# The experts' gates as one float32r product of N=256 per token, in place of three bf16 products

## The chip, the cores and the metric

The kernel runs on one core of one Trainium2 chip, as one program of some 47,000 recorded instructions. The metric is device time in microseconds from the program's start to its end; the time before is the median of three runs.

Names in what follows: PE is the TensorE (matrix products, results in PSUM), DVE the VectorE, ACT the ScalarE, POOL the GpSimd engine, SP the SyncE, which issues the loads of weights.

## The reference, cut to what matters

The program is one transformer block on 256 tokens: a modulated norm, a gated delta net and a sparse attention side by side, an output product, then a layer of 16384 small experts (PEER). The change lies in the last part alone:

```python
# 8 heads, 128 x 128 keys, 16 experts per head and token: 128 slots per token
s1 = einsum('thd,hkd->thk', qh[..., :half], keys1); v1, i1 = top_k(s1, 16)
s2 = einsum('thd,hkd->thk', qh[..., half:], keys2); v2, i2 = top_k(s2, 16)
sc, pos = top_k(v1[..., :, None] + v2[..., None, :], 16)      # over the 256 pairs
eidx = take_along_axis(i1 * 128 + i2, pos)                    # expert = (i, j)
gw = softmax(sc)                                              # the gates
act = gelu(einsum('td,thkd->thk', xb, u[eidx]))
out = einsum('thk,thkd->td', gw * act, v[eidx])
```

Only 128 of the 16384 experts have a gate that isn't zero for a given token.

## The kernel before

The kernel computes the activations of all 16384 experts densely, times a gate that is mostly zero, and then multiplies with all of v. Expert (i, j) lies in partition i, column j of two tiles A0 (j below 80) and A1 (the rest), each [128, js, 256 tokens].

*The loop over j (lines 1886 to 1901).* For each of 128 j, `stat256` makes 48 products of 128x256 on PE: 16 blocks of the model's width, three float32r passes each (the weights u in two parts, the activations in two parts). ACT applies gelu into A. The weights come through `Stream`, 512 KB a load, each load cut into two pieces of 128x512. ACT casts a piece to its high part `whi`, DVE subtracts to give the low part `wlo`; each piece feeds 12 products, so a j takes four. There are four buffers of each part (line 1636), and a piece is split when one is given out:

```python
stream = Stream(jobs2, 4, 4)                          # line 1636
S.copy(h[:, :n], r)                                   # advance(): whi
V.tensor_tensor(l[:, :n], r, h[:, :n], OP.subtract)   # wlo
```

*The gates (`gate_task`, lines 1827 to 1883)* run beside that loop, four tokens at a time in 64 batches. For a token t, G[i, j] = sum over the 128 slots of gate * [i = i_slot] * [j = j_slot]: a product over slots of two tables, `oi` (one where i is the slot's) and `ow` (the gate where j is the slot's). `make` builds the tables of a batch on DVE: two comparisons of 128x512 bf16 and three multiplications, since the gate is held in three bf16 parts whose sum is exact. `products` makes 12 products of 128x128 bf16, three accumulated per token. `put` multiplies the gates into the part of A that is there (DVE), and copies them to where activations are still to come (ACT); there the loop multiplies later (`aj`, lines 1896 to 1898).

*What sets the order.* The program is written out in one order by hand; each engine runs its own instructions in that order and waits on semaphores. `Background` advances generators between the products with u: after each three products `bg.step()` lets each chain go on if the planner's estimated time on PE (`times.free["P"]`) has come. `pause()` (line 1835) spaces a batch's four steps evenly over the time left until the loop's end less GEND = 20 us; a step yields a time, which is a lower bound beside the estimated end of the last instructions (plain), or the only condition (with a minus). After the loop `need("gates")` (line 1902) runs whatever steps are left, and only then the second half follows: products with v, whose left operand `wh`, `wl` is A split in two.

The routing before it (`route_task`) ends with the transposed tables of i, j and gate, slots in partitions, and the flag "gate", for which `gate_task` waits.

Of the kernel before, what the change touches and what calls it, by code (L numbers as in the profile page):

```python
# [18 lines left out]
T = 256  # L19
# [48 lines left out]
def _const_array():  # L68
# [19 lines left out]
    # inside chunks of 64, both of a block's by their rows  # L88
# [21 lines left out]
def _ktiled(w, width):  # L110
    """[K, N] -> flat, by column chunks of `width`: [N/width][K/256][128][2][width]"""
    K, N = w.shape
    return w.reshape(K // 256, 2, 128, N // width, width).transpose(3, 0, 2, 1, 4).reshape(-1)


def layout(i):
    """Arrays for the device: the inputs, laid out anew."""
# [61 lines left out]
# h comes in slices of its columns: the first block of 128, and how many  # L179
SLICES = [(0, 1), (1, 1)] + [(2 * i, 2) for i in range(1, 8)]  # L180
PART = "ma0 mb0 ma1 mb1 ma2".split()
ORDER = "vcvs h1 h2 h3 h4 h5 h6 h7 ma0 mb0 kskw vw ma1 mb2 mb1 ma2".split()   # under the delta net
CMP_AT = "h2 h3 h4 h5 h6 h7 kskw vw".split()
COVER_N = [["ma3"], ["mb3", "wg0"], ["wg1", "wg2"], ["wg3"]]    # under the sparse attention
# [6 lines left out]
class Times:  # L191
    """A rough estimate of when the instructions emitted so far will have run, in microseconds. It says only
    when a chain goes on between the long products; no result rests on it."""
# [3 lines left out]
    def __init__(self):  # L197
        self.free = dict.fromkeys([*"PVSGQD", "DQ"], 0.0)   # engines, the queue of loads, DMA, that for the queue
        self.by, self.ready, self.used = {}, {}, {}     # by tile: its writer, when it is written and was last used
        self.slots, self.array = {}, []  # L200
        self.mark, self.table = 0.0, 0
# [28 lines left out]
    def beside(self, lhsT, out):  # L230
        """in rows or columns of the array that the products just before leave free?"""
        r, c = lhsT.start_partition(), out.start_partition()
        new = r, r + lhsT.partition_size(), c, c + out.partition_size()
        if self.array and all(new[1] <= o[0] or o[1] <= new[0] or new[3] <= o[2] or o[3] <= new[2] for o in self.array):
            self.array.append(new)
            return True
        self.array = [new]
        return False
# [37 lines left out]
class Timed:  # L276
    """An engine whose instructions are noted in times."""
# [30 lines left out]
class Background:  # L308
    """Chains of short dependent steps, advanced between the long products: generators that yield where the
    next step needs the results of the last. What they yield, if anything, is a time to wait for besides, or,  # L310
    with a minus, instead."""

    def __init__(self, times, cap, fill, pace):
        """fill(): side work that waits for nothing; one piece of it each `pace()`"""
# [39 lines left out]
class Tokens:  # L354
    """Buffers that a chain may hold from one of its steps to another."""
# [13 lines left out]
class Lanes:  # L369
    """Sets of buffers, of which a chain takes one."""  # L370
# [13 lines left out]
def build(nc, tc, A, out, dump=None, stop=None):  # L384
    """dump(name, ap): a hook for debugging"""
# [17 lines left out]
def _build(nc, tc, A, out, stacks, dump, at, stop_at):  # L403
# [35 lines left out]
    banks = Tokens(6)       # of the 8: those that are held for longer than a step  # L439
# [8 lines left out]
    # ------------------------------------------------------------ the stream of weights  # L448
    class Stream:
        """Tiles of 128 x 1024 or less, loaded and given out in the order of jobs; a tile to be split comes  # L450
        as two halves, each in two float32r parts."""

        def __init__(self, jobs, nraw, nsplit, more=None, nmore=0, until=0):
            """jobs: (array, offset, elements by partition, pieces to be split, the step from one partition to
            the next if it isn't the elements'); 0 pieces: one that isn't split; for those before `until` there is also
            the room of nmore tiles in the pool `more`"""
# [7 lines left out]
            self.got = 0            # pieces given out  # L464
            # by pool: of how many tiles, and how many are loaded, neither split nor given out
            self.room, self.open_raw = [(self.raws, nraw), (more, nmore)], [0, 0]
            self.until = until
            self.open_cut = 0       # pieces split, not given out
            self.held = False       # the last piece given out is a raw tile
            self.hold = False       # split nothing for now  # L470
# [14 lines left out]
        def advance(self, busy):  # L485
            """busy: split pieces that are in use"""
            self.load()
            while len(self.ready) < len(self.pieces):
# [10 lines left out]
                r = self.raw[i][:, hf * n:(hf + 1) * n]     # the last of them frees it  # L499
# [10 lines left out]
        def get(self):  # L510
            """The next piece; the one before must have been used."""
# [15 lines left out]
    # ------------------------------------------------------------ constants  # L527
# [14 lines left out]
    mcol = cst.tile([128, 6, KT], F32, name="mcol")   # sh1, norm1_w (1 + sc1), g1, sh2, norm2_w (1 + sc2), g2  # L542

    modr = dram.tile([2, D], F32, name="modr")        # g1, g2
# [3 lines left out]
    # ------------------------------------------------------------ plan of the front's stream  # L548
# [7 lines left out]
    def jobs_ks(n, ks):  # L556
        """a pair of ks of a chunk, or one of them"""
# [3 lines left out]
    def jobs_ada(sl):  # L561
        """shift, then scale"""
# [4 lines left out]
    # shift, scale and gate of the first half, then of the second  # L567
    SH1, SC1, G1, SH2, SC2, G2 = range(6)
    cmp_left = [(A["cw1"], i * 128 * 1024, 1024, 0) for i in range(16)]
    # Until the whole of sh1 and sc1 is there, a slice of h is used as soon as it can be: for two chunks, whose  # L570
    # sums stay in PSUM, and for some of the mixers, whose sums go through DRAM. The tiles of ada for the next
    # slice come between those.
    LEAVE = SLICES[-1][0] // 2          # the first tile of a chunk that comes after
    jobs = jobs_ada(0)
    order = []                  # of the steps: (slice, chunk, ks) or "ada"
    for sl, (k0, nk) in enumerate(SLICES[:-1]):
# [6 lines left out]
        for i, n in enumerate(steps):  # L583
# [6 lines left out]
            else:  # L590
                order.append("ada")         # the end of the slice, by steps
# [5 lines left out]
    # after which tiles of which chunks one for the compressed keys and values comes  # L597
# [23 lines left out]
    # of W_out the last quarter in two: the less is left to do when the products are done  # L621
# [11 lines left out]
    st_f = stack()          # left: what the front keeps  # L633

    # the rest of what is loaded once
# [8 lines left out]
    # ------------------------------------------------------------ products in three float32r passes  # L644
# [3 lines left out]
    def dense(accs, lhi, llo, w, ks, first, last, name=None, ready=None):  # L648
        """accs[tb][128 tokens, w] = sum from the first k to the last of lhs^T(k, tb) weights(k, w)"""
# [19 lines left out]
    # ------------------------------------------------------------ ada  # L669
    def ada_tile(p, i, n, r):  # L670
        """p: rows 0, 32, 64, 96 add up to n blocks of 128 columns; the i-th tile of them"""
# [20 lines left out]
    def c_row(dst):  # L692
        """silu(c) in every partition"""
# [7 lines left out]
    def ada_late(parts, crow, acol, row, room):  # L701
        """parts of ada, by step 512 terms of 128 columns; crow(q): 512 of c's; room(m): where the m-th piece comes"""
# [39 lines left out]
    def ada_until(*parts):  # L742
        """the side work up to the end of some parts"""
# [8 lines left out]
    # ------------------------------------------------------------ h = norm(x) (1 + sc1) + sh1, transposed  # L752
# [110 lines left out]
    # ------------------------------------------------------------ gates, decays, rotary angles  # L863
# [12 lines left out]
    rc = per.tile([128, 2, 32], F32, name="rc")       # cos | cos  # L876
    rs = per.tile([128, 2, 32], F32, name="rs")       # -sin | sin
    gg = per.tile([128, 2, 8], F32, name="gg")
    Gc = per.tile([128, 2, 8], F32, name="Gc")        # cumulated g
    nGc = per.tile([128, 2, 8], F32, name="nGc")  # L880
    gam = per.tile([128, 2, 8], F32, name="gam")      # exp(G)
    bgm = per.tile([128, 2, 8], F32, name="bgm")      # beta exp(G)
    ekd = per.tile([128, 2, 8], F32, name="ekd")      # exp(G_end - G)
    ge = per.tile([128, 4, 8], F32, name="ge")        # exp(G_end) by chunk, in every partition
    kcT = per.tile([128, 2, 2, T], F32, name="kcT")   # k_c, v_c: [d, which, group, t]
    beta = sig[:, :, 8:16]
    # by head and chunk (of a block's two, one in each half of the partitions): exp(-|G_i - G_j|)
# [3 lines left out]
    def pre_task():  # L891
        # what is needed until E is written, in its place
# [18 lines left out]
        # angles brought into [-pi, pi]  # L911
# [23 lines left out]
        # g = -exp(A_log) softplus(a + dt_bias), cumulated inside chunks of 64  # L935
# [52 lines left out]
    def rope(dst, src, tb, n):  # L988
        """the first 32 of dst [128 t, n heads, 128] = those of src, rotated"""
# [13 lines left out]
    def kv_rot(a, o, dst, free):  # L1003
        """rotated and transposed columns [o, o + 256) of a chunk: dst [128 d, 2 groups, T]"""
# [19 lines left out]
    # ------------------------------------------------------------ gated delta net, a head at a time  # L1024
# [3 lines left out]
    # (I + L)^-T of a block, both chunks'; between them stays 0  # L1028
# [8 lines left out]
    def gdn_head(h, a):  # L1037
# [28 lines left out]
        # q and k stay as they are: 1 / |k| goes into the scales of what is made of them and into the rows of  # L1066
        # (I + L)^-1, which then gives U / |k| instead of U; 1 / |q| into the output's scale
# [981 lines left out]
```

## Time and profile before

| | |
|---|---|
| median of 3 runs (lowest, highest) | 2715.28 us (2714.2, 2716.81) |
| span of the profiled execution | 2713.1 us (no time of its own is given beside it) |
| PE, DVE, ACT busy | 99%, 72%, 51% of the span |
| loop over u | some 1161 to 1984 us |
| gates, first to last table and product | 1358.6 to 1913.4 us |
| products with v | from 1984.4 us |

The profile's views read here: the page's engine totals and its chain of work that ended last; windows (busy time of each engine in a stretch); groups of equal instructions with their mean duration; and timelines, in which the idle time ahead of an instruction stands in brackets with what ended it. A line number of a helper (L286) stands at nearly every instruction, so instructions are told apart by their tiles: `ps` is a PSUM bank, `ht` holds the activations h2. An instruction's duration reaches beyond the start of the next on its engine, so what one occupies is read from the distance of starts.

### The profile page before, as it was taken

How to read it: one execution, taken by the hardware profiler on the slowest of the kernel's cores; microseconds unless marked ns; L12 is line 12 of the kernel's file. 1: busy time of each engine (PE TensorE's matmuls, PEld its weight loads, DVE VectorE, ACT ScalarE, POOL GpSimd, SP SyncE). 2: the span in 40 equal slices, each digit the busy share in tenths (PEclk: the TensorE clock that was granted, in tenths of full speed). 3: DMA queues.
4: the chain of work that ended last, by engine and by line, in shares of the span. 5: the costliest groups of instructions: out<-in, count | busy, mean ns of one | idle time of the engine just before them, and what ended most of it. 6: DMA issues, size and time to landing. Idle time of an engine off the chain costs nothing.

```text
span 2713.1 us, 47110 instructions
## 1 busy us (share of the span) xinstructions
PE 2675.2 (99%) x17132; PEld 2275.8 (84%) x17132; DVE 1956.5 (72%) x4360; ACT 1389.9 (51%) x2966; POOL 35.2 (1%) x77
## 2 busy tenths in 40 slices
PE   7999999999999999999999999999999999999998
PEld 5777767777777777999999999999988888788886
DVE  6667877767777777899766666667577777766666
ACT  4446656555554445554544444444455555555555
POOL 0000000000000000000000000000000000000000
PEclk9999999999999999999999999999999999999999
DMA  9886756676676886566655555555577777766664
GB/s 345 311 314 213 223 166 202 209 235 218 208 238 203 306 301 210 188 180 186 184 159 157 154 156 156 156 155 156 174 250 234 235 236 236 255 188 187 188 189 158
DMA packets 176922, 571.12 MB, mean 211 GB/s; under 512 B 20049, under 2 KB 20385, under 8 KB 176177
## 3 DMA queue, kind: packets, MB, share of 16 engines
q1 hardware_dynamic: 168336, 538.18, 62.8%
q0 software_dynamic: 6624, 23.65, 2.5%
q10 hardware_dynamic: 1728, 6.29, 0.6%
q8 instruction: 134, 2.20, 0.3%
q14 instruction: 100, 0.81, 0.1%
HBM read 554.91 MB, written 13.13 MB: 209 GB/s over the span
## 4 chain that ended last, share of the span: by engine, by line
PE 93%; DVE 3%; DMA 2%; ACT 1%; issue 1%; DVEq 0%; ACTq 0%; POOLq 0%
PE ps L286 93%; DMA adas<-ada_t 1%; DVE wlo L286 1%; DVE adas L286 0%; DMA raw<-w_in 0%; ACT whi L286 0%; DVE x L286 0%; DVE ht L286 0%; DMA ccom<-consts 0%; DMA mix<-partd 0%; DVE big L286 0%; ACT P L286 0%; DMA mixd<-mix 0%; ACT ps L286 0%; ACT mix L286 0%
## 5 line engine op out<-in xcount | busy, mean ns | idle before, releaser
L286 DVE TENSOR_TENSOR wlo<-raw,whi 128x512 fp32r<-128x512 f32 (+2 forms) x1632 | 1099.8, 685 | 521.7 <-ACT whi L286 487.6
L286 ACT CAST whi<-raw 128x512 fp32r<-128x512 f32 (+2 forms) x1632 | 995.1, 618 | 778.8 <-PE ps L286 622.0
L286 PE MATMUL ps<-ht,whi 128*128 128x256 f32 x4608 | 828.8, 282 | 0.8 <-DVE ht L286 0.8
L286 PEld LDWEIGHTS ps<-ht,whi 128*128 128x128 f32 x4608 | 708.1, 189 | 1.2 <-DVE ht L286 1.0
L286 PE MATMUL ps<-ht,wlo 128*128 128x256 f32 x2304 | 647.2, 281 | 0.0
L286 PE MATMUL ps<-whi,ht 128*128 128x512 f32 (+2 forms) x1536 | 527.5, 402 | 4.4 <-ACT whi L286 2.7
L286 PEld LDWEIGHTS ps<-ht,wlo 128*128 128x128 f32 x2304 | 434.1, 188 | 0.0
L286 PE MATMUL ps<-wlo,wh 128*128 128x512 f32 x1024 | 406.0, 396 | 0.0
L286 PE MATMUL ps<-whi,wl 128*128 128x512 f32 x1024 | 405.0, 396 | 0.0
L286 PE MATMUL ps<-whi,wh 128*128 128x512 f32 x1024 | 402.6, 393 | 0.8 <-ACT wh L286 0.8
L286 PEld LDWEIGHTS ps<-whi,ht 128*128 128x128 f32 x1536 | 286.9, 188 | 91.2 <-issue 14.8
L286 PE MATMUL ps<-wlo,ht 128*128 128x512 f32 (+2 forms) x768 | 298.3, 388 | 2.2 <-DVE wlo L286 2.0
L286 PEld LDWEIGHTS ps<-whi,wh 128*128 128x128 f32 x1024 | 192.2, 188 | 48.9 <-ACT wh L286 1.0
L286 PEld LDWEIGHTS ps<-wlo,wh 128*128 128x128 f32 x1024 | 192.2, 188 | 47.0
L286 PEld LDWEIGHTS ps<-whi,wl 128*128 128x128 f32 x1024 | 192.2, 188 | 45.3 <-DVE wl L286 0.2
L286 ACT CAST wh<-A 128x256 fp32r<-128x256 f32 x256 | 103.9, 407 | 134.0 <-PE ps L286 134.0
L286 PEld LDWEIGHTS ps<-wlo,ht 128*128 128x128 f32 x768 | 145.2, 189 | 27.4 <-DVE wlo L286 4.9
L286 DVE TENSOR_TENSOR wl<-A,wh 128x256 fp32r<-128x256 f32 x256 | 108.8, 426 | 64.9 <-ACT wh L286 64.5
L286 DVE SCALAR_TENSOR_TENSOR adas<-adas,crow 128x512 f32<-128x512 f32 x192 | 131.4, 684 | 29.2 <-DMA adas<-ada_t 28.9
L286 PE MATMUL ps<-ow,oi 128*128 128x128 bf16 x768 | 101.3, 296 | 0.0
L286 ACT COPY A<-ps 128x192 f32<-128x192 f32 (+16 forms) x124 | 34.4, 307 | 114.0 <-DVE A L286 93.3
L286 PEld LDWEIGHTS <-oi 128*128 128x128 bf16 x768 | 81.7, 118 | 3.9
(320 smaller groups left out, 2307.3 us busy)
## 6 DMA issues: line engine op xcount, KB each, us to landing
raw<-u SPq DMA_DIRECT2D x256, 512.0 KB, 3.6
raw<-v SPq DMA_DIRECT2D x256, 512.0 KB, 3.6
raw<-w_in SPq DMA_DIRECT2D x170, 512.0 KB, 4.3
adas<-ada_t SPq DMA_DIRECT2D x192, 256.0 KB, 3.6
raw<-ada_w SPq DMA_DIRECT2D x64, 512.0 KB, 6.8
raw<-wn SPq DMA_DIRECT2D x32, 512.0 KB, 4.8
raw<-wo SPq DMA_DIRECT2D x32, 512.0 KB, 5.0
raw<-wq SPq DMA_DIRECT2D x32, 512.0 KB, 3.6
```

The lines of the kernel that those rows point to most:

```text
L286: r = f(*args, **kw)
```

## The change

The gate is now held in two parts, a float32r rounding and the rest, and both tables are float32r. For each token one product of N=256 gives the sums of both parts side by side, which then have to be added. In full:

- `make` builds the tables by token: `tensor_scalar` over a 128-column bf16 iota with the slot's i, j and gate parts as scalars per partition. That is one instruction for `oi` and two for `ow`, 12 of 128x128 per batch in two halves of two tokens, and four small ones per batch (`sl`, `gr`) that lay out the scalars. The tables have three buffers each, of two tokens.
- `products` makes four products of 128x256 float32r per batch, two tokens to a PSUM bank.
- `put` goes by two tokens: ACT copies one part from PSUM to the tile `gsum` (one buffer), DVE adds the other, and then the multiplication into A or the copies follow from `gsum`.
- The order of the steps in `gate_task` is written anew, four to a batch as before; the routing's split of the gate in three goes; `aj` has one buffer instead of two.

```diff
-    ij = [ep.tile([128, T], BF, name=f"ij{n}") for n in range(2)]
-    gs = [ep.tile([128, T], BF, name=f"gs{n}") for n in range(3)]
-    iota4 = ep.tile([128, 128, 4], BF, name="iota4")
+    ij = ep.tile([128, 2, T], BF, name="ij")
+    gs = ep.tile([128, T], F32, name="gs")
+    iotab = ep.tile([128, 128], BF, name="iotab")
...
         def make(t0):
-            oi = ep.tile([128, 128, nt], BF, name="oi", bufs=2)
-            ow = ep.tile([128, 3, 128, nt], BF, name="ow", bufs=2)
-            over = lambda a: a[:, None, t0:t0 + nt].to_broadcast([128, 128, nt])
-            V.tensor_tensor(ow[:, 2], iota4, over(ij[1]), OP.is_equal)
-            V.tensor_tensor(oi, iota4, over(ij[0]), OP.is_equal)
-            yield -pause()
-            for n in range(3):
-                V.tensor_tensor(ow[:, n], ow[:, 2], over(gs[n]), OP.mult)
-            ones[t0] = oi, ow
+            sl = ep.tile([128, 4, nt], F32, name="sl", bufs=2)
+            gr = ep.tile([128, nt], F32R, name="gr", bufs=2)
+            gt = gs[:, t0:t0 + nt]
+            V.tensor_copy(sl[:, 0:2], ij[:, :, t0:t0 + nt])
+            V.tensor_copy(gr, gt)
+            V.tensor_copy(sl[:, 2], gr)
+            V.tensor_tensor(sl[:, 3], gt, gr, OP.subtract)
+            ones[t0] = []
+            for i in range(nt // 2):
+                if i:
+                    yield -pause()
+                oi = ep.tile([128, 2, 128], F32R, name="oi", bufs=3)
+                ow = ep.tile([128, 2, 2, 128], F32R, name="ow", bufs=3)
+                for t in range(2):
+                    at = [sl[:, n, 2 * i + t:2 * i + t + 1] for n in range(4)]
+                    V.tensor_scalar(oi[:, t], iotab, at[0], None, op0=OP.is_equal)
+                    for n in range(2):
+                        V.tensor_scalar(ow[:, t, n], iotab, at[1], at[2 + n], op0=OP.is_equal, op1=OP.mult)
+                ones[t0].append((oi, ow))

         def products(t0):
-            for t in range(nt):
-                for n in range(3):
-                    PE.matmul(p[:, 128 * t:128 * t + 128], oi[:, :, t], ow[:, n, :, t], start=n == 0, stop=n == 2)
+            for oi, ow in ones.pop(t0):
+                p = ps()
+                for t in range(2):
+                    PE.matmul(p[:, 256 * t:256 * t + 256], oi[:, t], ow[:, t].rearrange("p n j -> p (n j)"),
+                              start=True, stop=True)
+                sums[t0].append(p)

         def put(t0):
-            pv = sums.pop(t0).rearrange("p (t j) -> p j t", t=nt)
...
+            for i, p in enumerate(sums.pop(t0)):
+                g = ep.tile([128, 128, 2], F32, name="gsum", bufs=1)
+                pv = p.rearrange("p (t n j) -> p n j t", t=2, n=2)
+                S.copy(g, pv[:, 1])
+                V.tensor_tensor(g, g, pv[:, 0], OP.add)
+                for q, (a, b) in enumerate(((0, JA), (JA, 128))):
+                    m = min(max(j_there, a), b)
+                    x = act_by[q][:, :, t0 + 2 * i:t0 + 2 * i + 2]
+                    if m > a:
+                        V.tensor_tensor(x[:, :m - a], x[:, :m - a], g[:, a:m], OP.mult)
+                    if m < b:
+                        S.copy(x[:, m - a:], g[:, m:b])
...
         for t0 in range(0, T, nt):
-            if t0 + nt < T:
-                yield from make(t0 + nt)
-                yield -pause()
+            new = make(t0 + nt) if t0 + nt < T else None
+            if new:
+                yield next(new)
             if t0:
                 put(t0 - nt)
             yield pause()
             products(t0)
+            yield -pause()
+            if new:
+                next(new, None)
             yield pause()
```

On DVE, a batch in the middle of the stage, before (A_11574 is A0; `ps` in the row on A is the bank of the gates' sums; `aj` is gelu's result where gates are there already):

```order
L286 TENSOR_TENSOR ow<-iota_11582,ij_11578 128x512
L286 TENSOR_TENSOR oi<-iota_11582,ij_11577 128x512
L286 TENSOR_TENSOR wlo<-raw,whi 128x512
L286 TENSOR_TENSOR ow<-ow,gs_11579 128x512
L286 TENSOR_TENSOR ow<-ow,gs_11580 128x512
L286 TENSOR_TENSOR ow<-ow,gs_11581 128x512
L286 TENSOR_TENSOR wlo<-raw,whi 128x512
L286 TENSOR_TENSOR A_11574<-A_11574,ps 128x47x4
L286 TENSOR_TENSOR A_11574<-A_11574,aj 128x40
```
And now, a first half of the tables with the put behind it; the second half of the tables stands between two later wlo:

```order
L286 CAST sl<-ij 128x8
L286 CAST gr<-gs 128x4
L286 CAST sl<-gr 128x4
L286 TENSOR_TENSOR sl<-gs,gr 128x4
L286 TENSOR_SCALAR oi<-iotab,sl 128x128
L286 TENSOR_SCALAR ow<-iotab,sl 128x128 x2
L286 TENSOR_SCALAR oi<-iotab,sl 128x128
L286 TENSOR_SCALAR ow<-iotab,sl 128x128 x2
L286 TENSOR_TENSOR gsum<-gsum,ps 128x256
L286 TENSOR_TENSOR A_11574<-A_11574,gsum 128x51x2
L286 TENSOR_TENSOR gsum<-gsum,ps 128x256
L286 TENSOR_TENSOR A_11574<-A_11574,gsum 128x51x2
```
What was a multiplication straight from PSUM is two additions and two multiplications behind six tables, with no wlo between them.

On ACT, the same place before, with the semaphores that each waits for:

```order
L286 ACTIVATE aj<-ps 128x40 [waits PE_49]
L286 ACTIVATE A_11574<-ps 128x216
L286 CAST whi<-raw 128x512 [waits DVE_49]
L286 COPY A_11574<-ps 128x31x4 [waits DVE_49]
L286 COPY A_11575<-ps 128x48x4
L286 CAST whi<-raw 128x512 [waits DMAHW3_49,PE_49,Activation_49]
```
And now:

```order
L286 CAST whi<-raw 128x512 [waits DMAHW1_49,DVE_49,PE_49]
L286 COPY gsum<-ps 128x256
L286 COPY A_11574<-gsum 128x36x2 [waits DVE_49]
L286 COPY A_11575<-gsum 128x48x2
L286 COPY gsum<-ps 128x256 [waits DVE_49,Activation_49]
L286 COPY A_11574<-gsum 128x36x2 [waits DVE_49]
L286 COPY A_11575<-gsum 128x48x2
L286 CAST whi<-raw 128x512 [waits PE_49]
```
Where one wait on DVE stood ahead of the next whi, three do, since the second copy into `gsum` has to wait until the first half is out of it.

On PE, the end of the products with u and the first with v, before:

```order
L286 MATMUL ps<-ht,whi 128x256 x2
L286 MATMUL ps<-ht,wlo 128x256
L286 MATMUL ps<-whi,wh 128x512
L286 MATMUL ps<-wlo,wh 128x512
L286 MATMUL ps<-whi,wl 128x512
```
And now:

```order
L286 MATMUL ps<-ht,whi 128x256 x2
L286 MATMUL ps<-ht,wlo 128x256
L286 MATMUL ps<-ow,oi 128x256 x32
L286 MATMUL ps<-whi,wh 128x512
L286 MATMUL ps<-wlo,wh 128x512
L286 MATMUL ps<-whi,wl 128x512
```
The products of the last eight batches (32 rows of `ow,oi`) have moved behind the last product with u. Between one batch's tables and the next, DVE has five wlo before and in turn 7, 7 and 6 now.

## Rows read from the trace of the kernel before

**Rows 1.** The page's part 1: busy us (share of the span) xinstructions
```profile
PE 2675.2 (99%) x17132; PEld 2275.8 (84%) x17132; DVE 1956.5 (72%) x4360; ACT 1389.9 (51%) x2966; POOL 35.2 (1%) x77
```

**Rows 2.** The page's part 4: chain that ended last, by engine
```profile
PE 93%; DVE 3%; DMA 2%; ACT 1%; issue 1%; DVEq 0%; ACTq 0%; POOLq 0%
```

**Rows 3.** Windows: us, busy us PE, PEld, DVE, ACT, POOL; clock, DMA, GB/s
```profile
1200.00:1270.00 70.00, 70.00 (x595) 70.00 (x594) 65.85 (x216) 34.23 (x63) 0.00 (x0) 1.00 0.62 180
...
1400.00:1500.00 100.00, 100.00 (x847) 99.26 (x846) 64.47 (x142) 44.71 (x111) 0.00 (x0) 1.00 0.53 155
```

**Rows 4.** Groups, 1357 to 1920 us: shapes, count, busy, mean ns
```profile
L286 PE MATMUL ps<-ow,oi 128*128 128x128 bf16 x768 | 101.3, 296 | 0.0
...
L286 DVE TENSOR_TENSOR ow<-ow,gs 128x512 bf16<-128x512 bf16 x192 | 75.4, 420 | 2.2
L286 DVE TENSOR_TENSOR ow<-iota,ij 128x512 bf16<-128x512 bf16 x64 | 27.0, 421 | 8.0 <-PE ps L286 6.8
L286 DVE TENSOR_TENSOR oi<-iota,ij 128x512 bf16<-128x512 bf16 x64 | 26.8, 419 | 0.0
```

**Rows 5.** Timeline of PE, u's end: start us, us, form, [idle <-releaser]
```profile
1983.37 0.28 PE L286 MATMUL ps<-ht,wlo 128*128 128x256 f32 x1
...
1984.42 0.51 PE L286 MATMUL ps<-whi,wh 128*128 128x512 f32 x1 [0.77 <-ACT wh L286]
```

**Rows 6.** Timeline of ACT, 1358 to 1411 us
```profile
1358.56 0.39 ACT L286 ACTIVATE A<-ps 128x256 f32<-128x256 f32 x1 [0.92 <-PE ps L286]
...
1364.24 0.39 ACT L286 ACTIVATE A<-ps 128x256 f32<-128x256 f32 x1 [0.92 <-PE ps L286]
...
1371.34 0.38 ACT L286 ACTIVATE A<-ps 128x256 f32<-128x256 f32 x1 [0.91 <-PE ps L286]
...
1409.76 0.51 ACT L286 COPY A<-ps 128x156 f32<-128x156 f32 x2 [0.99 <-DVE A L286]
1410.16 0.63 ACT L286 CAST whi<-raw 128x512 fp32r<-128x512 f32 x1
```

**Rows 7.** Timeline of DVE, 646 to 647 us
```profile
646.41 0.17 DVE L286 TENSOR_TENSOR sm<-sm,gates 128x6 f32<-128x6 f32 x1
646.61 0.48 DVE L286 TENSOR_SCALAR P<-P,sm 128x128 f32<-128x128 f32 x2
647.01 0.36 DVE L286 TENSOR_SCALAR Pc<-Pc,sm 128x15 f32<-128x15 f32 x2
```

**Rows 8.** Groups of DVE, whole span
```profile
L286 DVE TENSOR_TENSOR XY<-XY,ps 128x256 f32<-128x256 f32 x32 | 13.2, 416 | 6.0 <-PE ps L286 5.9
...
L286 DVE TENSOR_SCALAR P<-P,sm 128x256 f32<-128x256 f32 x32 | 9.7, 346 | 0.0
L286 DVE TENSOR_SCALAR h32b<-ps,mcol 128x256 f32<-128x256 f32 x16 | 8.6, 537 | 0.2 <-ACT ht L286 0.2
...
L286 DVE TENSOR_SCALAR h<-xnT,mcol 128x256 f32<-128x256 f32 x16 | 6.5, 407 | 0.0
```

**Rows 9.** Groups of ACT, whole span
```profile
L286 ACT COPY A<-ps 128x256 f32<-128x256 f32 x17 | 6.3, 373 | 10.6 <-PE ps L286 10.6
...
L286 ACT COPY A<-ps 128x52 f32<-128x52 f32 x3 | 0.6, 203 | 4.0 <-DVE A L286 4.0
```

**Rows 10.** Timeline of DVE, 1359 to 1411 us
```profile
1359.31 1.28 DVE L286 TENSOR_TENSOR wlo<-raw,whi 128x512 fp32r<-128x512 f32 x2
1360.52 1.21 DVE L286 TENSOR_TENSOR ow<-ow,gs 128x512 bf16<-128x512 bf16 x3
...
1409.41 0.32 DVE L286 TENSOR_TENSOR A<-A,ps 128x164 f32<-128x164 f32 x1
1410.83 0.69 DVE L286 TENSOR_TENSOR wlo<-raw,whi 128x512 fp32r<-128x512 f32 x1 [1.10 <-ACT whi L286]
```

**Rows 11.** Windows near the start, for the clock
```profile
20.00:24.00 4.00, 2.39 (x30) 1.72 (x18) 3.46 (x10) 2.60 (x6) 0.00 (x0) 1.00 0.92 282
24.00:28.00 4.00, 4.00 (x32) 2.66 (x34) 1.89 (x4) 1.53 (x4) 0.00 (x0) 0.57 0.99 351
```

More of the change, by code (lines that the diff above doesn't have):

```diff
@@ L1718, in _build @@
     gw = tmp(256).rearrange("p (b h s) -> p b h s", b=2, h=8)
-    gate = tmp(256)
     eidx = tmp(512).rearrange("p (w b n) -> p w b n", w=2, b=2)
-    ij = [ep.tile([128, T], BF, name=f"ij{n}") for n in range(2)]
-    gs = [ep.tile([128, T], BF, name=f"gs{n}") for n in range(3)]
-    iota4 = ep.tile([128, 128, 4], BF, name="iota4")
-    V.tensor_copy(iota4, C("iota")[:, :, None].to_broadcast([128, 128, 4]))
+    ij = ep.tile([128, 2, T], BF, name="ij")
+    gs = ep.tile([128, T], F32, name="gs")
+    iotab = ep.tile([128, 128], BF, name="iotab")
+    V.tensor_copy(iotab, C("iota"))
     MIN = -3.0e38
@@ L1788, in route_task @@
         yield bg.now() + RPACE
-        for dst, src in zip((*ij, gate), (eidx[:, 0], eidx[:, 1], gw.rearrange("p b h s -> p b (h s)"))):
+        for dst, src in zip((ij[:, 0], ij[:, 1], gs), (eidx[:, 0], eidx[:, 1], gw.rearrange("p b h s -> p b (h s)"))):
             S.copy(dst, transpose_to(ps(), src, 2).rearrange("p b t -> p (b t)"))
             yield bg.now() + RPACE
-        for n in range(3):
-            V.tensor_copy(gs[n], gate)
-            if n < 2:
-                V.tensor_tensor(gate, gate, gs[n], OP.subtract)
         done.add("gate")
@@ L1849, in make @@
-            ones[t0] = oi, ow
-        def products(t0):
-            oi, ow = ones.pop(t0)
-            p = ps()
-            for t in range(nt):
-                for n in range(3):
-                    PE.matmul(p[:, 128 * t:128 * t + 128], oi[:, :, t], ow[:, n, :, t], start=n == 0, stop=n == 2)
-            sums[t0] = p
+            sl = ep.tile([128, 4, nt], F32, name="sl", bufs=2)
+            gr = ep.tile([128, nt], F32R, name="gr", bufs=2)
+            gt = gs[:, t0:t0 + nt]
+            V.tensor_copy(sl[:, 0:2], ij[:, :, t0:t0 + nt])
@@ L1859, in put @@
+        def products(t0):
+            sums[t0] = []
+            for oi, ow in ones.pop(t0):
[4 more added lines that the diff above has]
+                sums[t0].append(p)
         def put(t0):
             nonlocal t_there
-            pv = sums.pop(t0).rearrange("p (t j) -> p j t", t=nt)
-            for q, (a, b) in enumerate(((0, JA), (JA, 128))):
-                m = min(max(j_there, a), b)
-                x = act_by[q][:, :, t0:t0 + nt]
-                if m > a:
-                    V.tensor_tensor(x[:, :m - a], x[:, :m - a], pv[:, a:m], OP.mult)
-                if m < b:
-                    S.copy(x[:, m - a:], pv[:, m:b])
+            for i, p in enumerate(sums.pop(t0)):
[10 more added lines that the diff above has]
+                        S.copy(x[:, m - a:], g[:, m:b])
@@ L1869, in put @@
             t_there = t0 + nt
-        yield from make(0)
+        first = make(0)
+        next(first)
+        next(first, None)
         yield pause()
         for t0 in range(0, T, nt):
-            if t0 + nt < T:
-                yield from make(t0 + nt)
-                yield -pause()
+            new = make(t0 + nt) if t0 + nt < T else None
+            if new:
+                yield next(new)
             if t0:
@@ L1895, in _build @@
         if n:
-            t = ep.tile([128, T], F32, name="aj", bufs=2)
+            t = ep.tile([128, T], F32, name="aj", bufs=1)
             act(t[:, :n], p[:, :n], AF.Gelu_apprx_tanh)
```

## The prediction

> **What bounds the kernel now.** The page's first part comes first: PE is busy in 99% of the span [rows 1], and the chain that ended last runs through PE for 93% of it [rows 2]. So time is PE's time, plus whatever makes PE wait. The windows say the same of the stage that changes: from 1400 to 1500 us PE is busy throughout, DVE for 64 us, ACT for 45 [rows 3]. The row of 1200 to 1270 us, the routing, is a warning and a comfort: DVE 94% busy there, and PE still without a gap. The groups of that stage then give what is to go: 768 bf16 products, and 320 table instructions on DVE that take 75.4 + 27.0 + 26.8 = 129 us [rows 4]. The end of the stage is read last: from the last product with u to the first with v 1.05 us pass [rows 5].
>
> **What is removed on PE.** ACT's activations of one j end a row of 48 products each. Without gates between them they start 5.68 us apart (1358.56, 1364.24), with one batch of gates 7.10 (1371.34) [rows 6]. So a product with u takes 5.68 / 48 = 0.118 us, and a batch of four tokens 1.42 us. 64 batches: -90.9 us.
>
> **What is added on PE.** Four products a batch of the same form as those with u (128x256, float32r, weights float32r): 4 x 0.118 = 0.47 us. The order of the changed program has 56 batches' products among those with u and 8 behind the last of them: 56 x 0.47 = +26.5 us.
>
> **What is added on DVE, and whom it holds.** A batch now makes 12 tables of 128x128 by a scalar per partition. The nearest rows: with one such scalar and 128 elements the second starts 0.48 - 0.28 = 0.20 us after the first; 15 elements 0.36 - 0.23 = 0.13 to 0.14 [rows 7]. A second scalar adds 407 - 346 = 61 ns (256 elements, one and two scalars) [rows 8]. So 0.20 for an oi and 0.26 for an ow, 1.46 for a half of the tables (two tokens: 2 oi, 4 ow). Bounds: below, 0.14 each, as the 15 elements; above, one element a cycle, as the 256 from PSUM that take 537 - 407 = 130 ns more [rows 8], 65 ns more for 128. I take the middle, since P<-P,sm is the same operation on 128 float32 in SBUF. The four small instructions that split the gate cost 0.43: two at 0.08, one that waits for its predecessor at 0.20 as the small pair of [rows 7], one more 0.08.
>
> The put is in two halves now, and they share one gsum tile. From the first add's start: add 0.45 (416 ns and the wait for its end [rows 8]), ACT's copies into A0 and A1 0.10 + 0.24 (58 and 96 elements, by the 203 ns of 52 and the 373 of 256 [rows 9]; the one after starts 0.10 before the end, as two take 0.51 and whi behind them starts at 0.40 [rows 6]), only then gsum's second copy 0.03 + 0.37 [rows 9], add 0.03 + 0.42, copies 0.03 + 0.10 + 0.14, and then the next whi 0.62 + 0.04: 2.6 us until DVE can begin the next wlo. The wait at its end is there before too: 1.10 us behind each put, while ACT copies and casts [rows 6, 10], and PE had no gap there [rows 3].
>
> Is it still? There are four buffers of whi. The whi ahead of a batch of tables can be cast when PE has read the piece four before. From that product: its own end 0.28 [rows 5], handover 0.04, whi 0.62, handover 0.04, wlo until the next instruction 0.60 (two wlo in 1.21 [rows 10]), small ones 0.43, half the tables 1.46, put 2.6, wlo and handover 0.74: 6.8 us. In that time PE has one more product of that piece, four pieces of 12, two products of the fifth that want whi alone, and four of the gates: 55 x 0.118 = 6.5 us. PE waits 0.3 us. Where a j's activation (aj, then A, 0.36 us on ACT) comes ahead of that whi, or behind the put, it is 0.75 and 0.65. The order repeats these three kinds (7, 7 and 6 pieces between one batch and the next, five before), so 0.57 on average: 56 x 0.57 = +32 us. DVE in all is not full: 6.7 wlo at 0.60, tables 2.9, small ones 0.4, aj 0.4, adds and products 1.3, some 9.1 us of a batch's 10; it is the one chain, not the sum, that PE waits for.
>
> **What is moved behind the loop.** The steps are spaced by the planner's estimate, a step goes on only when the planner believes its inputs done, and with the new instructions it reaches 56 batches where 64 did fit. Seven batches of tables and eight puts stand after the last product with u, where nothing covers them: 14 half tables at 1.46, 7 splits at 0.43, 8 puts at 2.24 (two adds at 0.45, two pairs of products on A of 160 and 96 elements at 0.24 + 0.18, by the 0.32 us of 164 [rows 10] less 0.08 that the next overlaps, 0.43 for gsum's second copy, 0.07 for the end that it waits for), 0.5 at the very end: 41.8 us. wh and the first product with v follow as before, so +41.5.
>
> **The clock.** PE has four products in some 5.6 us there. At 24 to 28 us the granted clock was 0.57, so mostly its lower level (1.2 of 2.4 GHz), after a stretch in which PE was busy for 2.39 of 4 us [rows 11]: 43% of 4 us lost. +2 us once, when v begins. Everything else keeps its place: ACT's added copies (0.37 twice, two more small ones, some 1 us a batch) fit in its idle half, the loads have 47% of their time free [rows 3], and the single aj buffer is read long before the next j.
>
> **Sum.** -90.9 + 26.5 + 32 + 41.5 + 2 = +11 us. The trace's execution has a span of 2713.1 us and no time of its own beside it; the median of the runs, 2715.3, is 2.2 above. So 2724 as a span, 2726 us as a median.
>
> **The skill against the row.** Two wlo of 512 columns in a row start 0.60 apart and a 128-column table by a scalar 0.20, so a quarter of the columns costs a third of the time [rows 10, 7]. The Trainium skill, "VectorE: DVE Perf Modes", section "The TRN2 errata — SBUF-src ops pay a fixed extra latency per instruction", says that a fixed cost falls on each instruction and advises tiles of 512 elements or more, which speaks against 12 small tables in place of five large ones. Its table gives 58 + FD/Accel cycles, an estimate of 0.127 us for a table at two elements a cycle; by that the halves cost 0.76, PE would not wait, the tail would be 32 us and the sum -31. The trace speaks against that figure: 0.20 with one scalar [rows 7].
>
> **Rivals.**
> - *The cover holds.* Tables at the lower bound, 0.14: a half costs 0.84, 0.62 less, and the 0.57 of waiting is gone; the tail is 8 to 9 us shorter. -90.9 + 26.5 + 33 + 2 = -29, 2686 us. With tables at 0.20 and 0.26 but a wait that doesn't come about (a handover or a cast of ACT earlier than I have it), -21, 2694 us. For it: PE without a gap beside a DVE that is 94% busy [rows 3]. Against: there no put stands between. It decides, and the change gains, from a wait under 0.37 us a batch down (11 / 56 = 0.2 less than I have).
> - *Tables at one element a cycle.* Half a table 1.85: 0.39 more of waiting in each of 56 batches, 22 us, and 5.5 more in the tail: +39, 2754 us. For it: bf16 in and float32r out is a pair that no row of a scalar operation shows. Against: both sides lie in SBUF, as with P<-P,sm, whose 256 elements take 346 ns where the PSUM form less its second scalar takes 537 - 61 = 476 [rows 8].
> - *All of the 64 us on PE are gained*, the rest hidden: 2651 us. The order speaks against it: nothing on PE stands beside the eight last puts.
>
> **Chances.** My forecast 0.48 (own range 2708 to 2744, a wait of 0.25 to 0.9 a batch), cover 0.27, one a cycle 0.22, all gained 0.03. Below 2709.9 (0.2%, about what can be told from no change) fall the cover, the last and little of the forecast: 0.30. Within 0.2%, from the forecast's lower part: 0.15. Slower: 0.55. Range 2694 to 2760: from the cover without cheaper tables to one element a cycle with some more in the tail.
>
> **What would show it.** Right: PE's gaps in the stage are one a batch, of some half a microsecond, ended by DVE's wlo behind the second put; whi idle for gsum or A; the u stage ends without gates some 42 us before v begins, with PE idle and DVE full; the 128x256 gates 0.47 a batch. The row of oi and ow gives the tables: about 0.28 and 0.34 us as durations, 0.20 and 0.26 apart. Wrong: no gaps in the stage (then 2694 or less), tables 0.33 apart (2754), or a tail that is much shorter than 36 or longer than 48 us.

## The result: slower, by almost four times the step forecast

The changed kernel takes 2755.8 us (median of 4 runs, 2752.9 to 2757.1) against 2714.7 us before (2713.9 to 2716.8): ratio 1.0148, 95% interval 1.0135 to 1.0161. Slower was the likeliest side of the forecast and the time lies in its range, but the step is +41 us where +11 was forecast. The profiled execution has a span of 2755.3 us against 2713.1, so 42.2 us are to be found.

### The profile after

The page's first part and its chain, as in [rows 1, 2]:

```profile
PE 2660.2 (97%) x16620; PEld 2234.9 (81%) x16620; DVE 2090.2 (76%) x5296; ACT 1434.6 (52%) x3174; POOL 35.4 (1%) x77
...
PE 79%; DVE 12%; ACT 5%; DMA 2%; issue 1%; ACTq 0%; DVEq 0%; POOLq 0%
```

PE is listed 15 us less busy, and its share of the chain is 14 points lower, with 9 more for DVE and 4 for ACT. Where, the windows show (us, then busy us of PE, of PEld, which is the loading of weights into PE, of DVE, ACT, POOL; granted clock, DMA share, GB/s), beside 100.00, 99.26 and 64.47 of PE, PEld and DVE in [rows 3]:

```profile
1400.00:1500.00 100.00, 94.69 (x762) 91.04 (x761) 81.54 (x258) 52.45 (x146) 0.00 (x0) 1.00 0.50 159
...
1980.00:2030.00 50.00, 21.89 (x44) 12.98 (x45) 40.39 (x166) 10.23 (x28) 0.00 (x0) 0.52 0.18 66
```

PE now has gaps all through the stage, and behind it a stretch where DVE works and PE hardly does, mostly at the lower of the two clock levels (granted clock 0.52). The waits of PE from 1360 to 2030 us (us in total, times, longest); before, the same stretch has the last kind alone, 0.8 us:

```profile
PE ps L286 <- DVE ow L286: 23.1, 15, 3.0
PE ps L286 <- ACT whi L286: 15.1, 35, 0.7
PE ps L286 <- DVE wlo L286: 12.1, 54, 0.2
PE ps L286 <- ACT wh L286: 4.9, 1, 4.9
```

The groups that take the place of [rows 4] (1357 to 1978.2 us; count | busy, mean ns | idle before):

```profile
L286 DVE TENSOR_SCALAR ow<-iotab,sl 128x128 fp32r<-128x128 bf16 x456 | 136.5, 342 | 0.0
L286 DVE TENSOR_SCALAR oi<-iotab,sl 128x128 fp32r<-128x128 bf16 x228 | 64.0, 281 | 0.0
...
L286 PE MATMUL ps<-ow,oi 128*128 128x256 f32 x225 | 35.9, 281 | 0.0
```

So far this is what the forecast named: tables of 281 and 342 ns, a tail, two kinds of wait. The sizes are read from starts. In 35 of the 54 batches that wait, it looks so on PE (start us, us, form, [idle <-releaser]):

```profile
1970.46 0.40 PE L286 MATMUL ps<-ht,whi 128*128 128x256 f32 x2
1970.70 0.27 PE L286 MATMUL ps<-ht,wlo 128*128 128x256 f32 x1
1971.43 0.51 PE L286 MATMUL ps<-ht,whi 128*128 128x256 f32 x2 [0.45 <-ACT whi L286]
1972.16 0.38 PE L286 MATMUL ps<-ht,wlo 128*128 128x256 f32 x1 [0.22 <-DVE wlo L286]
1972.38 0.63 PE L286 MATMUL ps<-ow,oi 128*128 128x256 f32 x4
```

Products in a row start 0.118 us apart. The pair with whi was due at 1970.82 and starts at 1971.43, 0.61 late, where the row says 0.45. The one with wlo was due 0.24 later and comes 0.73 later: 0.49 lost, where the row says 0.22. The idle times add up to 27 us in the stage; start to start, over all 4455 products with u and 56 batches of gates, 56.7 us are lost, all in 54 of the batches: 54 x 0.49 = 26.4 at wlo, 35 x 0.59 = 20.7 at whi, 19 x 0.21 = 3.9 at a whi for which no idle time is listed, and 54 x 0.11 = 5.7 ahead of the gates behind such a wait. Before, the same sum over the stage is 0.5 us.

What holds PE there, on ACT and on DVE, same stretch:

```profile
1965.67 0.62 ACT L286 CAST whi<-raw 128x512 fp32r<-128x512 f32 x1
1966.18 0.39 ACT L286 COPY gsum<-ps 128x256 f32<-128x256 f32 x1
1969.22 0.20 ACT L286 COPY A<-gsum 128x4 f32<-128x4 f32 x1 [2.66 <-DVE gsum L286]
1969.80 0.37 ACT L286 COPY gsum<-ps 128x256 f32<-128x256 f32 x1 [0.38 <-DVE A L286]
1970.66 0.20 ACT L286 COPY A<-gsum 128x4 f32<-128x4 f32 x1 [0.49 <-DVE gsum L286]
1970.76 1.66 ACT L286 CAST whi<-raw 128x512 fp32r<-128x512 f32 x3
```

```profile
1966.32 0.69 DVE L286 TENSOR_TENSOR wlo<-raw,whi 128x512 fp32r<-128x512 f32 x1 [0.22 <-ACT whi L286]
1966.93 0.17 DVE L286 CAST sl<-ij 128x8 f32<-128x8 bf16 x1
...
1967.35 0.28 DVE L286 TENSOR_SCALAR oi<-iotab,sl 128x128 fp32r<-128x128 bf16 x1
...
1968.77 0.41 DVE L286 TENSOR_TENSOR gsum<-gsum,ps 128x256 f32<-128x256 f32 x1
...
1971.41 1.89 DVE L286 TENSOR_TENSOR wlo<-raw,whi 128x512 fp32r<-128x512 f32 x3 [0.26 <-ACT whi L286]
```

ACT copies into gsum at once, then stands for 2.66 us, since DVE has half the tables ahead of the add; three casts of whi are queued behind. From that whi (1965.67) to PE's product with the next wlo (1972.16) it is 6.49 us.

The end of the stage, against [rows 5]:

```profile
1978.05 0.28 PE L286 MATMUL ps<-ht,wlo 128*128 128x256 f32 x1
1978.17 0.63 PE L286 MATMUL ps<-ow,oi 128*128 128x256 f32 x4
...
2017.19 1.20 PE L286 MATMUL ps<-ow,oi 128*128 128x256 f32 x2 [2.52 <-DVE ow L286]
2023.26 0.79 PE L286 MATMUL ps<-whi,wh 128*128 128x512 f32 x1 [4.88 <-ACT wh L286]
2023.85 0.63 PE L286 MATMUL ps<-wlo,wh 128*128 128x512 f32 x1
```

And the stage's beginning, the row that stands at 1364.24 in [rows 6]:

```profile
1366.83 0.39 ACT L286 ACTIVATE A<-ps 128x256 f32<-128x256 f32 x1 [0.92 <-PE ps L286]
```

With these, the 42.2 us divide (each a difference of two starts):

| stretch | before | after | change | forecast |
|---|---|---|---|---|
| up to that activation | 1364.2 | 1366.8 | +2.6 | 0 |
| from it to the last product with u | 619.1 | 611.2 | -7.9 | -32.4 |
| from there to the first product with v | 1.05 | 45.2 | +44.2 | +41.5 |
| from there to the end | 728.7 | 732.0 | +3.4 | +2 |

The first row is no effect of the change that could be found: on PE the programs are alike there, and the activation ahead of it (1358.56 before, 1361.15 after) lies anywhere from 1355.4 to 1362.1 in the profiled runs below.

### The profile page after: what moved, and what is told of

It reads as the page before. It is cut to its first block, busy times and chain, and to the rows that moved or that the text cites. A ratio compares the mean times of both kernels' runs of the same rounds, so it can differ in the third digit from the quotient of the medians.

```text
span 2755.3 us, 47258 instructions
## 1 busy us (share of the span) xinstructions
PE 2660.2 (97%) x16620; PEld 2234.9 (81%) x16620; DVE 2090.2 (76%) x5296; ACT 1434.6 (52%) x3174; POOL 35.4 (1%) x77
## 4 chain that ended last, share of the span: by engine, by line
PE 79%; DVE 12%; ACT 5%; DMA 2%; issue 1%; ACTq 0%; DVEq 0%; POOLq 0%
PE ps L286 79%; DVE wlo L286 4%; DVE ow L286 2%; ACT whi L286 2%; DVE gsum L286 2%; DMA adas<-ada_t 1%; DVE oi L286 1%; ACT gsum L286 1%; DVE A L286 1%; ACT A L286 1%; DVE sl L286 1%; DMA raw<-w_in 0%; DVE adas L286 0%; ACT aj L286 0%; DVE ht L286 0%
## 5 line engine op out<-in xcount | busy, mean ns | idle before, releaser
L286 PEld LDWEIGHTS ps<-ht,whi 128*128 128x128 f32 x4608 | 706.2, 188 | 28.0 <-ACT whi L286 26.9
L286 PEld LDWEIGHTS ps<-ht,wlo 128*128 128x128 f32 x2304 | 434.0, 188 | 23.2 <-DVE wlo L286 23.2
L286 PEld LDWEIGHTS ps<-wlo,ht 128*128 128x128 f32 x768 | 144.9, 189 | 26.4 <-DVE wlo L286 3.9
L286 DVE TENSOR_SCALAR ow<-iotab,sl 128x128 fp32r<-128x128 bf16 x512 | 153.2, 342 | 0.0
L286 ACT COPY A<-gsum 128x96 f32<-128x96 f32 (+38 forms) x166 | 37.5, 262 | 175.1 <-DVE gsum L286 175.1
L286 DVE TENSOR_TENSOR gsum<-gsum,ps 128x256 f32<-128x256 f32 x128 | 53.6, 418 | 34.5 <-ACT gsum L286 34.5
```

The lines of the kernel that those rows point to most:

```text
L286: r = f(*args, **kw)
```

## The experiments

### Without the tail

```
-        for t0 in range(0, T, nt):
-            new = make(t0 + nt) if t0 + nt < T else None
+        for t0 in range(0, T - 8 * nt, nt):
+            new = make(t0 + nt) if t0 + nt < T - 8 * nt else None
...
-        put(T - nt)
+        put(T - 9 * nt)
```

> Leaves out the gates of the last 32 tokens (eight batches); all instructions before them stand in the same order. Theory (of 42 us, the uncovered tail is 45.1 and the start of v at a low clock some 1.4 more than nothing, and the stage under u gains 3 to 4 net): the tail and half the clock's loss go, with the last batch's four products under u: 2756 - 45.1 + 1.0 (wh's split before v, as before) - 0.5 - 2 = 2709 us, so 5 us faster than before. Rival 1 (the tail was mostly filled with work that would stand there anyway, or its price comes back in v): 2730 or more. Rival 2 (the tail is 41.5 as forecast and the stage's loss lies elsewhere, such as slow float32r products behind v's start): 2714 or more with the stage under u unchanged.

Measured: 2708.6 us, ratio to before 0.9966 (0.9954 to 0.9978). PE at the end of the stage:

```profile
1977.53 0.28 PE L286 MATMUL ps<-ht,wlo 128*128 128x256 f32 x1
1978.63 0.51 PE L286 MATMUL ps<-whi,wh 128*128 128x512 f32 x1 [0.83 <-ACT wh L286]
```

The stage ends where it did, 0.5 us apart, and v begins 44.6 us sooner: the tail with what it does to v's start costs 47 us, as the theory had it; both rivals fall.

### The gate products ahead of the tables

```
             new = make(t0 + nt) if t0 + nt < T else None
+            products(t0)
             if new:
                 yield next(new)
...
             yield pause()
-            products(t0)
             yield -pause()
```

> A batch's four gate products are issued ahead of the next batch's tables and the put, instead of behind them. Theory (the forecast counted these four products, 0.47 us, into the cover of the chain, and they stood behind it): waits of PE under u fall from 0.91 to 0.44 us a batch, 56 x 0.47 = 26 us; tail and all else unchanged: 2756 - 26 = 2730 us. Rival 1 (PE's wait is set by ACT, which holds whi behind A<-gsum while DVE makes tables, whatever PE has in hand): no change, 2750 to 2757, and the rows of PE's waits stay 35 and 54. Rival 2 (it is the sum of DVE's work, not the chain): no change as well.

Measured: 2736.1 us, ratio to before 1.0074 (1.0057 to 1.0091), 20 us under the changed kernel. PE's waits in the stage:

```profile
PE ps L286 <- DVE wlo L286: 12.0, 54, 0.2
...
PE ps L286 <- ACT whi L286: 0.2, 1, 0.2
```

The 35 waits for whi are gone, though ACT is held as long as before, so four products more in hand do cover them; both rivals fall. Of the 26 us expected 20 came. The 54 waits at wlo stay at 0.49 each, start to start: PE still comes up to a piece just when its whi is cast, and wlo follows whi 0.72 later while PE has 0.24 to do. The lost sum is 38.3 us in place of 56.7. The forecast's three kinds show where the missing six went (18 batches of each, start to start): 0.80, 1.25 and 1.10 in the changed kernel, 0.73, 0.78 and 0.62 here. Two kinds fell by the four products; the first did not, since its chain grew, from whi to PE's wlo 6.53 in the changed kernel and 6.93 here. The whi and DVE's pair of wlo in such a batch, in the changed kernel and then here (the second wlo of the pair is that whi's):

```profile
1558.80 0.62 ACT L286 CAST whi<-raw 128x512 fp32r<-128x512 f32 x1 [0.35 <-PE ps L286]
1558.77 1.39 DVE L286 TENSOR_TENSOR wlo<-raw,whi 128x512 fp32r<-128x512 f32 x2
```
```profile
1551.55 0.62 ACT L286 CAST whi<-raw 128x512 fp32r<-128x512 f32 x1 [0.35 <-PE ps L286]
1551.99 1.29 DVE L286 TENSOR_TENSOR wlo<-raw,whi 128x512 fp32r<-128x512 f32 x2
```

Here DVE comes to the pair from the other half of the tables 0.44 after the whi has begun, so that DVE's earlier work, and no longer the whi alone, sets when the chain starts.

### The put ahead of the tables

```
-            if new:
-                yield next(new)
             if t0:
                 put(t0 - nt)
+            yield -bg.now()
+            if new:
+                next(new)
             yield pause()
             products(t0)
```

> Only the put and the first half of the next batch's tables change places; DVE's row of work between two wlo stays as long, and the gate products stay behind PE's wait. Theory (the chain runs through ACT too: whi can't be cast before DVE has made the tables and ACT's copies of the put are out): now ACT casts the next whi while DVE makes the tables, so the last 0.66 us of the chain (whi and its handover) stand beside it: waits from 0.91 to some 0.3 us a batch, 2756 - 0.6 x 56 = 2722 us, and the whi rows of PE's waits go. Rival (DVE's row of work alone sets the wait): 2750 to 2757.

Measured: 2716.7 us, ratio to before 1.0004 (0.9994 to 1.0013), 39 us under the changed kernel and all the loss under u but for 21 us. The row of DVE's work is as long as it was:

```profile
1800.90 0.69 DVE L286 TENSOR_TENSOR wlo<-raw,whi 128x512 fp32r<-128x512 f32 x1 [0.73 <-ACT whi L286]
1801.51 0.41 DVE L286 TENSOR_TENSOR gsum<-gsum,ps 128x256 f32<-128x256 f32 x1
...
1805.82 2.49 DVE L286 TENSOR_TENSOR wlo<-raw,whi 128x512 fp32r<-128x512 f32 x4
```
```profile
1803.82 1.66 ACT L286 CAST whi<-raw 128x512 fp32r<-128x512 f32 x3
```

But at its end four wlo go without a wait, since ACT got its casts in (the last row) while DVE made the tables, and no wait of PE for whi is left. The chain went through ACT; the rival falls.

### The tables made once

```
+                if t0:
+                    ones[t0].append(kept[i])
+                    continue
                 oi = ep.tile([128, 2, 128], F32R, name="oi", bufs=3)
```

> The tables are made for the first four tokens alone, and all batches' products use them (the gates are then wrong from the fifth token on); the splits of the gates, products and puts stay. It gives PE's part alone. Theory: the float32r products take 0.118 us each, DVE has time, all batches stand under u, and the waits and the tail go but for a put or two: 2713 - 96 (old gates, 64 x 1.5) + 64 x 0.58 + 1 = 2655 us, within 8. Rival (the products themselves or the additions with their waits hold PE, not the tables): 2690 or more.

Measured: 2657.1 us, ratio 0.9782 (0.9766 to 0.9798). The stage from 1400 to 1900 us, in the order of the windows above:

```profile
1400.00:1900.00 500.00, 500.00 (x4229) 500.00 (x4228) 354.36 (x948) 295.55 (x798) 0.00 (x0) 1.00 0.58 176
```

PE has no gap there, with all 64 batches under u. This is what the change gives on PE, 60 us, when nothing waits; the products and the additions cost nothing beside.

### All steps on their pace

```
-            yield pause()
+            yield -pause()
```
(both places in the loop)

> The steps of the gates go on by the clock of their pace alone, not when the planner believes their inputs done. All 64 batches stand under u, in smaller portions: one or two wlo between a half of the tables and the put more often. Theory (chain and tail): the tail's 45 and v's clock 2 to 3 go, eight more batches of products cost 8 x 0.58 = 4.6, and the waits per batch fall, as portions with a wlo between are shorter: with none left 2756 - 48 + 5 - 51 = 2662, with half of them (0.45 x 64 = 29) 2691. Rival (the sum of DVE's work is the bound: its busy time under u would be 518 + 8 x 5.6 = 563 us, as much as PE's 563): waits of 0.9 us a batch stay, 2756 - 48 + 5 + 7 = 2720.

Measured: 2861.4 us, ratio 1.0529 (1.0512 to 1.0547). Neither theory. PE, PEld, DVE and clock in two stretches:

```profile
1600.00:1700.00 100.00, 77.72 (x478) 69.64 (x477) 84.95 (x311) 40.65 (x134) 0.00 (x0) 0.86 0.30 91
...
1900.00:2000.00 100.00, 100.00 (x848) 100.00 (x847) 56.60 (x89) 48.42 (x88) 0.00 (x0) 1.00 0.61 185
```

The pace is in the planner's time, and that, as the code has it, runs on when the planned PE waits; the plan itself was not looked at, so this part is argued. What the rows show is that the batches did not spread: the last tables were made at 1846 us, 286 us ahead of the last product with u. Until then the program has 33 products with u and 2.7 wlo to a batch, where the changed kernel has 80 and 6.7. Start to start, a batch's own instructions take 4.8 us of DVE (tables 2.8, splits 0.4, put 1.4, aj 0.1) and its wlo 1.6; with 1.2 of waits that is 7.6, the batches' distance, for what takes PE 33 x 0.118 + 0.47 = 4.4. So DVE, its waits included, is the bound, and 64 x 3.2 = 205 us are lost on PE; at such waits (up to 2.5 us) the clock fell too. The expectation took for granted that a step's due time would hold on the chip.

### Spread by a count of products, with and without fewer splits

```
-        start, steps = bg.now(), 0
-        pace = ((128 - j_there) * 5.15 - GEND) / (4 * T / nt)
+        start, steps = ks_there, 0          # products with u so far, by three
+        pace = (16 * (127 - j_there) - 24 - start % 16) / (4 * T / nt + 4)
...
-            return start + steps * pace
+            while ks_there < start + steps * pace and j_there < 127:
+                yield
...
+            if t0 < T:
+                products(t0)
             for i in range(2):          # half the tables, half the put, twice
```

> The steps are spread evenly over the products with u by a count of the products instead of the planner's time: half the tables, half the put, half the tables, half the put, each some 1.6 pieces of whi apart, the gate products ahead of the tables. All 64 batches stand under u. DVE's work a batch is the same: 6.7 x 0.60 + 2.92 + 0.43 + 1.8 + 0.6 = 9.8 of PE's 10.0 us. Theory (chain and tail; the sum of DVE's work still fits): the tail's 45 and v's clock 2 to 3 go, 8 more batches' products add 4.6, the waits of 51 mostly go: 2756 - 48 + 5 - 51 = 2662, up to 2675 with 0.2 us a batch left; the kernel that leaves the tables out took 2657. Rival (DVE is the bound at such a density, as in the run with the steps on their pace): 2690 to 2720, with PE's waits at wlo in most batches.

Measured: 2729.5 us, ratio 1.0054 (1.0037 to 1.0071). The tail is gone, but the waits are not: 2729.5 lies above even the rival's 2690 to 2720, and the place is not the rival's either. PE waits at the gate products (34.5 us listed for ow, 4.0 for wlo).

The second kernel adds only this, for 16 tokens at a time where it was four:

```
+            if t0 % 16 == 0:
+                sl = ep.tile([128, 4, 16], F32, name="sl", bufs=2)
```

> As the spread steps, and the four small instructions that split the gates are done for 16 tokens at a time: 0.3 us less of DVE a batch. Theory (chain and tail): no wait is set by DVE's sum, so 0 to 5 us less than the spread steps alone, 2658 to 2670. Rival (DVE's sum is the bound): 64 x 0.3 = 19 us less than the spread steps alone.

Measured: 2700.0 us, ratio 0.9944 (0.9928 to 0.9961), 29 us less by the medians and 22 by the spans of the profiled executions (2720.1 and 2697.9 us; the first is the fastest of that kernel's four runs, which go up to 2730.9). The 48 x 4 small instructions that went take 48 x 0.43 = 21 of DVE's time. So what DVE saves comes off the time, as the rival says. But DVE isn't full of work. PE's waits from 1360 to 2030 us, then DVE's from 1400 to 1900, in that kernel:

```profile
PE ps L286 <- DVE ow L286: 26.0, 29, 2.0
```
```profile
DVE wlo L286 <- ACT whi L286: 46.3, 93, 1.2
```

46 us of DVE's 500 go in waits for whi, which stands on ACT behind an A<-gsum that waits for DVE.

### Spread, with both orders turned

```
+            if t0:
+                put(t0 - nt, 0)
+            if new:
+                next(new)                # half the tables
+            yield from pause()
+            if t0:
+                put(t0 - nt, 1)
+            if t0 < T:
+                products(t0)
+            yield from pause()
+            if new:
+                next(new, None)          # the other half
+            yield from pause()
```

> Spread by the count of products as before, splits for 16 tokens at a time, and three steps a batch: half the put and then half the tables; half the put and then the gate products of tables made four pieces of whi earlier; half the tables. Theory (what was left in the two spread runs are two orders: A<-gsum holds ACT, and with it whi, while DVE makes the tables queued ahead of the add, 46 us of idle DVE at wlo; and PE comes to the gate products before their tables are there, 26 us): both orders are turned, so the waits fall from 32 to 44 us to under 15: 2657 + 0 to 15, so 2657 to 2675. Rival (DVE's sum with its fixed gaps is full at 9.4 of 10.0 us a batch, whatever the order): 2695 to 2705, as the run with the splits for 16 tokens.

Measured: 2672.0 us (median of 5), ratio to before 0.9838 (0.9824 to 0.9851): 45 us faster than before, 84 than the change as it was. Waits of PE and of DVE in the same stretches:

```profile
PE ps L286 <- DVE wlo L286: 9.1, 17, 1.1
PE ps L286 <- ACT wh L286: 0.8, 1, 0.8
```
```profile
DVE wlo L286 <- ACT whi L286: 22.3, 58, 0.7
```

Half of DVE's waits went, and all of PE's at the gates. Both orders were turned at once, so what each is worth alone is not shown. What is left to the 2657 us of the tables made once is 15 us, with DVE busy for 93% of the stage, so a sum of DVE's work that is full at 2700 us is refuted.

## Why the prediction was right in kind and wrong in size

- **Removed on PE, added on PE: right.** 768 products of 0.118 us went, 224 of 0.118 came; the tables made once give the 60 us.
- **The tables' price: right.** An oi to the next start 0.20, an ow 0.26, a half 1.42 (1967.35 to 1968.77; 1.46 forecast). The rival of one element a cycle forecast 2754, nearly the time that came, and is refuted by this row: the number fits, the mechanism doesn't. The forecast's estimate of 0.127 us, worked out from the Trainium skill's table in "VectorE: DVE Perf Modes", section "The TRN2 errata — SBUF-src ops pay a fixed extra latency per instruction", fails here too.
- **The chain: right.** The forecast's terms from the whi to PE's wlo (6.8 less the product's end and its handover) are 6.49 us, the rows give 6.49, through ACT, and the run with the put first shows that ACT's part counts. That both agree to the last digit is luck: over all 54 waits it is 6.47 to 6.94, on average 6.63.
- **What PE has meanwhile: wrong, the step that failed.** "... two products of the fifth that want whi alone, and four of the gates: 55". The four gate products are not in hand. They stand behind the first product with the wlo that PE waits for: in the rows above the gates start at 1972.38, right after the wait. So PE has 51 products, 6.0 us, and every kind of wait is 0.47 longer: 0.77, 1.22 and 1.12, where 0.3, 0.75 and 0.65 were forecast. Measured: 0.81 in the 19 batches without a listed wait for whi (0.49 + 0.21 + 0.11), 1.19 in the other 35 (0.59 + 0.49 + 0.11); by the three kinds 0.80, 1.25 and 1.10. The sum is 56.7 us in place of 32, +24.7 of the 31 that were missing. The order of the instructions showed it, and moving those four products gave back 20 us.
- **The tail: right in kind, 2.7 short.** The put of the last batch under u falls behind the loop as well: nine puts, not eight, at 2.24.
- **The clock: right in kind, 1.4 short.** The granted clock was 0.56 from 2023 to 2030 us, v's first stretch; with the rest of v +3.4, where +2 was forecast.
- The remaining +2.6 lies ahead of the stage, in what both programs have alike on PE.
- That the time lies in the stated range is luck: the forecast's own range ended at 2744 us and its own wait at 0.9 a batch, where 2755.8 and 1.05 came, and the range reached to 2760 for the sake of the rival whose mechanism is refuted.

Two sentences of "what would show it" misled as well: the gaps are one stretch a batch, but ended by whi first in 35 of 54, and their listed lengths, 0.22 and 0.45, look like the "half a microsecond" of the forecast when they cost 1.0. The Trainium skill bears on this, "Perfetto Trace Analysis", section "Identifying the Most-Contended Engine": for the distance from the engine's limit, busy matmuls are a poor measure as they are pipelined, the busy share of weight loads a better one. The trace agrees: from 1400 to 1900 us PE's busy share fell by 4.8 points (500.00 to 476.21 us), that of weight loads by 7.7 (496.40 to 457.87), and 56.7 of 611 us are 9.3%.

## What to carry to other kernels

When a chain is weighed against the work that an engine has in hand, go through that engine's order product by product: what stands behind the instruction that waits covers nothing. A long piece of work on one engine is dear not by its length alone but by who is queued behind its consumer, so put what another engine's queue waits for ahead of it: that gave 39 us with the work as long as before. And spread side work by a count of the main work: due times in planned time bunched here. The count alone took away the tail; the waits went down with the orders turned.

## What the runs showed of the hardware

- A stall of PE costs more than its listed idle time: 0.61 and 0.49 us start to start for 0.45 and 0.22. Of each, 0.16 is that the end of a product is listed 0.28 behind its start while the next may start after 0.118; and the product behind one that waited starts 0.22 after it, not 0.118 (the gates at 1972.38, behind 1972.16). The late piece is the weights of these products, and the idle time listed ahead of their loading, 26.9 + 23.2 = 50 us where PE lists 27, comes near the 56.7 that are lost:

```profile
L286 PEld LDWEIGHTS ps<-ht,whi 128*128 128x128 f32 x4608 | 706.2, 188 | 28.0 <-ACT whi L286 26.9
L286 PEld LDWEIGHTS ps<-ht,wlo 128*128 128x128 f32 x2304 | 434.0, 188 | 23.2 <-DVE wlo L286 23.2
```

- Behind a table of 128 columns from bf16 to float32r, both in SBUF, the next instruction starts after 0.20 us with one scalar and after 0.26 with two: 60 ns for the second scalar at 128 columns (281 and 342 ns), 61 at 256 [rows 8].
- Stalls of about 1 us every 11 left the granted clock at 1.00 (1400 to 1900 us); in the run on pace, with PE busy 75 to 78 of 100 us, it was 0.86 to 0.90 (1400 to 1800 us), and in the tail 0.50 (1984 to 1991 us). In the run spread by a count, with waits of up to 2.2 us at the gates, it was 0.97 (1400 to 1900 us).
